# The first head's scores and exponentials are emitted beside the last projection, and the ring of exponentials moves into a pool that stays open

## The chip, the cores and the metric

The kernel runs on one core of one Trainium2 chip. The metric is device time in microseconds (us) of one launch. Instructions run on TensorE (PE, and PEld for its weight loads), VectorE (DVE), ScalarE (ACT) and GpSimd (POOL); SyncE (SP) issues nearly all transfers. Each engine runs its own instructions in order, and waits where an operand, a buffer or a transfer isn't ready.

## The reference, cut to what matters

```python
xn = rmsnorm(x, mix_norm);  proj = xn @ w_in          # 2 sequences x 512 tokens, 1024 -> 3072 columns
q, k, v, u = ...                                      # attention: 8 heads x 64; Hyena: 3 x 512 channels
q, k = rope(rmsnorm_f32(q, q_norm)), rope(rmsnorm_f32(k, k_norm))
attn = dilated_attention(q, k, v)                     # three (window, dilation) branches, merged by softmax
hy = hyena_mixer(u, ...)                              # short conv, then two gated long convolutions by FFT
mixed = concat(rmsnorm(attn), rmsnorm(hy));  h = x + mixed @ w_out
y = h + square(relu(rmsnorm(h, ffn_norm) @ w_up)) @ w_down
```

## The kernel before

All is float32 in value. A product is made of three matmuls of rounded halves (`hi`, `lo`), which `mm3` on line 91 emits; `act` on line 67 and `tt` on line 70 are the helpers under which most ACT and DVE work is recorded.

The first part of the program is written as Python generators which `interleave` merges by rough costs that each of them yields. One stream makes the filters of the Hyena group; two streams (`HA`, `HB`) run the Hyena convolutions, each as forward transforms (`psf`), a product on DVE (`t`, `yh`, `yl`), inverse transforms (`psi`) and a combination on DVE and POOL (`sm`, `wsb`, `u`, `z`); one stream runs the projections `proj_u` and `proj_qkv` (`psq`) and after them the attention; the last one turns the result of Hyena into `h` (`w_out_hyena`, `psm` and `psw`). A scheduler that knows the program's dependencies then fixes each engine's order.

The last projection is that of v for the second half of the heads (stream key `Q21`, `which` = 2, `half` = 1). Its q, k and v go to memory in DRAM (`q_d`, `k_d`, `v_d`). Only when it has ended are the pools `lw` and `la` (its weights and the normed input) closed, and `rm` and `lb` (attention) opened over their place: `start_attention` then loads the bias table, and `attn_load` loads q, k and v of a pair of heads (`qin`, `vin`).

For a head n = 2j + h, `stage_t` transposes its q and k (`psk`, 4 transposes each) and splits them (`qk`); `stage_a` makes the 128 x 512 scores of one tile of queries (`pss`, 2 matmuls), adds the bias and takes the maximum on DVE (`pe`, `mx`), and ACT makes exponentials in place; `stage_b` turns one block of keys (`psp`, 4 transposes, and `ph`, `pl`); `stage_v` multiplies by v (`pv`); `stage_c` turns the result back (`po`). `attention` runs five tiles of scores ahead of the rest:

```python
        for n in range(2):
            for k in range(2):
                stage_t(n, k)
        ...
        for t in range(5):
            scores()
```

Scores wait in a ring of eight buffers of 128 x 512 in `lb` (tag `pe`). When the second Hyena stream has stored its last result (`hy_d`), `w_out_hyena` loads it back in pieces (`hyr`), turns them (`psm`), and loads the weights of the output projection (`wur`).

Of the kernel before, what the change touches and what calls it, by code (L numbers as in the profile page):

```python
# [8 lines left out]
F32 = mybir.dt.float32  # L9
F32R = mybir.dt.float32r  # L10
# [45 lines left out]
def hybrid_encoder_kernel(ctx: ExitStack, tc: tile.TileContext, i: dict, outs, dbg=None):  # L56
# [74 lines left out]


    la, la_close = open_pool("la")
    lw, lw_close = open_pool("lw")
# [35 lines left out]
    def norm_x(s):  # L170
        for t in range(4):
            x = xs[s, t]
            c = slice(4 * s + t, 4 * s + t + 1)
            junk = [lw.tile([128, 512], F32, name="junk", tag=("y", "ut")[k], bufs=2) for k in range(2)]
            lo, hi = x[:, :512], x[:, 512:]
            nc.vector.tensor_tensor_reduce(out=junk[0], in0=lo, in1=lo, scale=1.0, scalar=0.0,
                                           op0=ALU.mult, op1=ALU.add, accum_out=rsc[:, 0, c])
            act(junk[1], hi, AF.Square, accum_out=rsc[:, 1, c])
            tt(nc.vector, ssx[:, c], rsc[:, 0, c], rsc[:, 1, c], ALU.add)
            rstd(ssx[:, c], ssx[:, c], D)  # L180
            act(hi, hi, AF.Copy, scale=ssx[:, c])
            nc.vector.tensor_scalar(lo, lo, ssx[:, c], None, op0=ALU.mult)
            yield 0, 1.2, 0
        for d in range(8):
            ps = bank("pst", "hx")
            for t in range(4):
                nc.tensor.transpose(ps[:, t * 128:(t + 1) * 128], xs[s, t][:, d * 128:(d + 1) * 128], ident)
            act(xh[s][:, d], ps, AF.Copy, scale=col(R_MIX + d))
            stt(xl[s][:, d], ps, col(R_MIX + d), f32(xh[s][:, d]), ALU.mult, ALU.subtract)
            if s == 0 and d == 3:  # L190
                load_x(1, nc.scalar, tc.keep_in_program_order)
            yield 0.43, 0.66, 0


    def load_w(src, first=False):

        out = []
        for k in range(src.shape[1]):
# [174 lines left out]
    def proj_u(q, w=None):  # L373
# [4 lines left out]
        def turn(s, a, y):  # L378
            pt = bank("pst", "tr", [128, 4, 128])
            for t in range(4):  # L380
                nc.tensor.transpose(pt[:, t], y[:, t * 128:(t + 1) * 128], ident)  # L381
            ut = lw.tile([128, 4, 128], F32, name="ut", tag="ut", bufs=2)
            act(ut, pt)
# [136 lines left out]
    def rope_tables():  # L520
        cs = lw.tile([128, 4, 2, 32], F32, name="cs", tag="y", bufs=2)
        nc.sync.dma_start(cs, i["c_rope"])
        g = lw.tile([128, 2, 64], F32, name="g", tag="ut", bufs=2)
# [4 lines left out]
        ng = lw.tile([128, 2, 64], F32, name="ng", tag="ut", bufs=2)  # L528
        nc.gpsimd.tensor_scalar(ng, g, -1.0, None, op0=ALU.mult)
# [8 lines left out]
    def proj_qkv(which, half):  # L538

        w = [(hi[:, c:c + 256], lo[:, c:c + 256]) for hi, lo in load_w(w_qkv[which, half]) for c in (0, 256)]  # L540
        for mp in range(4):
            s, t0 = divmod(2 * mp, 4)
# [8 lines left out]
            if which == 2:  # L551
# [3 lines left out]
                continue  # L555
            sq = lw.tile([128, 2, 256], F32, name="sq", tag="ut", bufs=2)
            rr = lw.tile([128, 8], F32, name="rr", tag="rr", bufs=3)
# [21 lines left out]

    ab = lw.tile([128, 4, 4, 64], F32, name="ab")  # L580
    w0 = load_w(w_u[0], first=True)
# [206 lines left out]
    PAIRS = [(s, 2 * g + p) for g in range(2) for s in range(NSEQ) for p in range(2)]  # L788
    split, po_of, den_of, sta, exps = {}, {}, {}, {}, {}

    def stage_t(n, k):


        j, h = divmod(n, 2)
        ps = bank("psk", "tr")
        for t in range(4):
            lined(nc.tensor.transpose(ps[:, t * 128:(t + 1) * 128], split[j][k][:, t, h], ident))  # L797
        hi = lb.tile([128, 512], F32R, name="qk", tag="qk", bufs=QKB)
        act(hi, ps)
# [3 lines left out]
        else:  # L803
            lo = lb.tile([128, 512], F32R, name="qk", tag="qk", bufs=QKB)
            tt(nc.vector, lo, ps, f32(hi), ALU.subtract)
            sta[n, k] = hi, lo

    def stage_a(n, t):

        j, h = divmod(n, 2)  # L810
        if t == 0:
            if h == 0:
                den_of[j] = lb.tile([128, 4, 2], F32, name="den", tag="den", bufs=2)
            exps[n] = [lb.tile([128, 4], F32, name="mx", tag="mx", bufs=3)]
# [5 lines left out]
        nc.vector.tensor_tensor_reduce(out=e, in0=ps, in1=bias[:, 384 - 128 * t:896 - 128 * t], scale=1.0, scalar=3e38,  # L820
                                       op0=ALU.add, op1=ALU.min, accum_out=mx[:, t:t + 1])
# [62 lines left out]
    def attention():  # L884
        load_pair(0)
        load_pair(1)
        for n in range(2):
            for k in range(2):
                stage_t(n, k)
                yield 0.4, 0.6, 0  # L890
        ahead = [(n, t) for n in range(NI) for t in range(4)]

# [4 lines left out]

        for t in range(5):
            scores()
            yield 0.47, 1.0, 0  # L900

# [29 lines left out]
    def w_out_hyena():  # L931
# [4 lines left out]
        for s in range(NSEQ):  # L936
# [6 lines left out]
            for t in range(4):  # L943
# [132 lines left out]
    w_out_part(1, between)  # L1076
    rm_close.close()
    hnB, hnB_close = open_pool("hnB")
    hn_pool(hnB, 1)
# [383 lines left out]
```

## Time and profile before

| | us |
|---|---|
| median of three runs (lowest, highest) | 1302.66 (1301.4, 1307.25) |
| the profiled execution, device time | 1303.84 |
| its span, first to last instruction | 1302.1 |
| PE busy in the span | 1263.6 (97%) |
| DVE, ACT, POOL busy | 1008.8, 658.5, 151.4 |

A busy PE is one with a matmul in flight; matmuls overlap, so the time between starts is the cost of one. Idle time of PE is mostly in three places: the first 60 us, the passage from the projections to the attention (432 to 480 us), and short gaps later. A row of the timeline merges equal instructions (x4) and ends, in brackets, with the idle time before them and what ended it.

### The profile page before, as it was taken

Reading aid. Unit: us, or ns where it says so; the run is one execution under the profiler, and the core shown is the slowest. Engines: PE = TensorE matmul, PEld = TensorE weight load, DVE = VectorE, ACT = ScalarE, POOL = GpSimd, SP = SyncE. Lnnn points to the kernel's source line nnn. Section 1 sums busy time; section 2 is a strip of 40 time slices with the busy share of each in tenths; the row PEclk is TensorE's granted clock in tenths of the full one; section 3 lists DMA queues with packets and bytes.
Section 4 is the critical chain, followed back from the end, with each engine's and each line's share of the span. In section 5 each row is a group of like instructions: output and inputs, shape, how many; then the busy total and the mean of one; then the engine's idle time right before and its main releaser. Section 6 shows DMA issues by size and latency. Waiting matters only on the chain.

```text
span 1302.1 us, 19021 instructions
## 1 busy us (share of the span) xinstructions
PE 1263.6 (97%) x6837; PEld 1079.8 (83%) x6837; DVE 1008.8 (77%) x1601; ACT 658.5 (51%) x1501; POOL 151.4 (12%) x131
## 2 busy tenths in 40 slices
PE   6999999999999889999999999999999999999998
PEld 5688889999999768788777888888887888887887
DVE  6787668898887777877569887887857688578885
ACT  6445434564564586768657444333335654334350
POOL 2110001443342130003031000000000000001000
PEclk9999999999999899999999999999999999999999
DMA  6545433444453494334232555444447853473323
GB/s 239 191 136 171 145 110 104 116 103 141 121 121 81 143 290 148 105 121 163 82 129 83 173 172 162 146 155 145 137 165 265 291 160 114 162 259 92 87 70 124
DMA packets 166275, 192.83 MB, mean 148 GB/s; under 512 B 42715, under 2 KB 106115, under 8 KB 166180
## 3 DMA queue, kind: packets, MB, share of 16 engines
q1 hardware_dynamic: 164740, 185.05, 45.0%
q0 software_dynamic: 864, 4.46, 0.9%
q10 hardware_dynamic: 576, 2.10, 0.4%
q8 instruction: 54, 0.88, 0.3%
q14 instruction: 41, 0.34, 0.1%
HBM read 126.82 MB, written 64.75 MB: 147 GB/s over the span
## 4 chain that ended last, share of the span: by engine, by line
PE 81%; DVE 9%; ACT 4%; DMA 3%; issue 2%; POOL 1%; SPq 0%; DVEq 0%; ACTq 0%; POOLq 0%
PE pu L91 24%; PE pn L91 19%; PE psu L91 10%; PE psq L91 6%; PE psw L91 5%; PE psf L91 4%; PE psi L91 3%; PE pv L845 2%; PE pss L818 2%; PE psp L831 2%; DVE clo L70 1%; DMA hyr<-hy_d 1%; PE pst L381 1%; DVE t L70 1%; PE psk L797 1%
## 5 line engine op out<-in xcount | busy, mean ns | idle before, releaser
L91 PE MATMUL pu<-hn,chl 128*128 128x512 f32 x768 | 184.6, 390 | 2.0 <-POOL hn L70 2.0
L91 PEld LDWEIGHTS pu<-hn,chl 128*128 128x128 f32 x768 | 144.2, 188 | 32.3 <-POOL hn L70 2.4
L91 PE MATMUL pn<-hn,chl 128*128 128x512 f32 x576 | 141.4, 392 | 1.0 <-ACT chl L67 1.0
L91 PEld LDWEIGHTS pn<-hn,chl 128*128 128x128 f32 x576 | 108.7, 189 | 24.8 <-ACT chl L67 1.9
L67 ACT ACTIVATE chi<-fa 128x1024 fp32r<-128x1024 f32 x49 | 51.9, 1060 | 124.4 <-PE pu L91 63.0
L91 PE MATMUL psq<-wlo,xh 128*128 128x256 f32 x384 | 108.8, 283 | 0.4 <-DVE wlo L70 0.4
L91 PE MATMUL psq<-whi,xl 128*128 128x256 f32 x384 | 108.7, 283 | 0.0
L91 PE MATMUL psq<-whi,xh 128*128 128x256 f32 x384 | 108.6, 283 | 0.0
L70 DVE TENSOR_TENSOR clo<-fa,chi 128x1024 fp32r<-128x1024 f32 x49 | 61.2, 1248 | 39.4 <-ACT chi L67 39.4
L91 PE MATMUL pu<-chi 128*128 128x512 f32 x248 | 86.6, 398 | 2.0 <-DVE chi L70 1.1
L91 PE MATMUL pu<-clo,chi 128*128 128x512 f32 x200 | 78.2, 391 | 1.6 <-DVE clo L70 1.6
L91 PE MATMUL pn<-chi 128*128 128x512 f32 x228 | 79.1, 389 | 0.0
L67 ACT ACTIVATE chl<-tmp 128x512 fp32r<-128x512 f32 x64 | 40.2, 630 | 76.0 <-PE pu L91 46.1
L91 PE MATMUL psu<-xh,whi 128*128 128x512 f32 x192 | 77.6, 407 | 0.5 <-ACT xh L67 0.5
L91 PE MATMUL pu<-chi,clo 128*128 128x512 f32 x200 | 77.8, 389 | 0.0
L91 PE MATMUL psf<-ih,dft 128*128 128x256 f32 x384 | 77.0, 283 | 0.2 <-ACT ih L67 0.2
L91 PE MATMUL psu<-xl,whi 128*128 128x512 f32 x192 | 76.7, 400 | 0.0
L91 PE MATMUL psu<-xh,wlo 128*128 128x512 f32 x192 | 76.1, 396 | 0.0
L91 PE MATMUL pn<-clo,chi 128*128 128x512 f32 x192 | 74.9, 390 | 0.1
L91 PE MATMUL pn<-chi,clo 128*128 128x512 f32 x192 | 74.7, 389 | 0.0
L91 PEld LDWEIGHTS psq<-wlo,xh 128*128 128x128 f32 x384 | 73.7, 192 | 0.6 <-DVE wlo L70 0.6
L91 PEld LDWEIGHTS psq<-whi,xh 128*128 128x128 f32 x384 | 73.7, 192 | 0.0
(243 smaller groups left out, 3201.5 us busy)
## 6 DMA issues: line engine op xcount, KB each, us to landing
fa<-f_d SPq DMA_DIRECT2D x49, 512.0 KB
wur<-in_w_up_t_dram SPq DMA_DIRECT2D x32, 512.0 KB
f_d<-x SPq DMA_DIRECT2D x60, 256.0 KB
wd<-in_w_down_dram SPq DMA_DIRECT2D x14, 1024.0 KB
f_d<-s SPq DMA_DIRECT2D x45, 256.0 KB
wraw<-in_w_u_dram SPq DMA_DIRECT2D x24, 256.0 KB
u_d<-ut SPq DMA_DIRECT2D x24, 256.0 KB
z<-u_d SPq DMA_DIRECT2D x24, 256.0 KB
```

The source lines that it names most:

```text
L67: nc.scalar.activation(out, in_, func, **kw)
L70: eng.tensor_tensor(out, a, b, op=op)
L91: pin(nc.tensor.matmul(ps, lhsT=w, rhs=x, start=start and k == 0, stop=stop and k == n - 1))
L381: nc.tensor.transpose(pt[:, t], y[:, t * 128:(t + 1) * 128], ident)
L797: lined(nc.tensor.transpose(ps[:, t * 128:(t + 1) * 128], split[j][k][:, t, h], ident))
L818: lined(nc.tensor.matmul(ps, lhsT=sta[n, 0][:, t * 128:(t + 1) * 128], rhs=kk, start=e == 0, stop=e == 1))
L831: lined(nc.tensor.transpose(ps[:, t * 128:(t + 1) * 128], exps[n][1 + t][:, kt * 128:(kt + 1) * 128], ident))
L845: lined(nc.tensor.matmul(pvs[n], lhsT=w, rhs=x, start=kt == 0 and e == 0, stop=kt == 3 and e == 1))
```

## The change

Head 0 is taken out of `attention` and given a stream of its own, `X`, with the generator `early`. It may start as soon as the last projection's weights are loaded (key `W21`). It loads q and k of heads 0 and 1 head by head (128 x 2 x 128 elements a transfer, where a pair's were 128 x 2 x 256), transposes head 0 and makes its four tiles of scores and exponentials. The bias is loaded twice: `bias0` for head 0 early, and `bias` as before. The attention's streams then begin with the transposes of head 1 and one tile of its scores. For pair 0, `attn_load` loads only v.

The buffers for this come from a new pool `le`, opened ahead of `la` and `lw`. It takes over the tags `wraw` (4 buffers), `ut` (2) and the table `ab` (the place of 2), and is closed only after the output projection. The ring of eight exponentials lies in these places (`exp_tile`), and the ring in `lb` is gone.

```diff
@@ pools
+    le, le_close = open_pool("le")
     la, la_close = open_pool("la")
@@ load_w
-                   lw.tile([128, 512], F32, name="wraw", tag="wraw", bufs=4))
+                   le.tile([128, 512], F32, name="wraw", tag="wraw", bufs=4))
...
@@ proj_qkv
+        done.add(f"W{which}{half}")
@@ attn_load
-        ins = []
-        for name, src in (("qin", q_d), ("qin", k_d)):
+        ins = [None, None] if (s, p) == PAIRS[0] else []
+        for name, src in (("qin", q_d), ("qin", k_d))[len(ins):]:
@@
+    def early():
+        bias0.append(le.tile([128, 896], F32, name="bias0", tag="ab", bufs=1))
+        den_of[0] = den0
+        for h in range(2):
+            for k, src in enumerate((q_d, k_d)):
+                t = le.tile([128, 4, 2, 64], F32, name="qin", tag="wraw", bufs=4)
+                for m in range(2):
+                    nc.sync.dma_start(t[:, 2 * m:2 * m + 2].rearrange("p t d e -> p t (d e)"),
+                                      src[m, :, 0, :, h].rearrange("p a d e -> p a (d e)"))
+                raws[h, k] = t.rearrange("p t d e -> p t (d e)")
+            if h == 0:
+                nc.sync.dma_start(bias0[0], i["c_bias"])
+        for k in range(2):
+            stage_t(0, k)
+            yield 0.4, 0.6, 0.6
+        for t in range(4):
+            stage_a(0, t)
+            yield 0.47, 1.0, 0.5
+
+    def exp_tile(i):
+        i %= 8
+        if i < 6:
+            tag, bufs = (("ut", 2), ("wraw", 4))[i > 1]
+            return le.tile([128, 512], F32, name="pe", tag=tag, bufs=bufs)
+        if i == 6:
+            two[:] = [le.tile([128, 2, 512], F32, name="pe", tag="ab", bufs=1)]
+        return two[0][:, i - 6]
@@ stage_a
-        ps = bank("pss", "ss")
+        ps = bank("pss", "ss" if n else "tr")
...
-        e = lb.tile([128, 512], F32, name="pe", tag="pe", bufs=8)
+        e = exp_tile(4 * n + t)
@@ attention
-        for n in range(2):
-            for k in range(2):
-                stage_t(n, k)
-                yield 0.4, 0.6, 0
-        ahead = [(n, t) for n in range(NI) for t in range(4)]
+        for k in range(2):
+            stage_t(1, k)
+            yield 0.4, 0.6, 0
+        ahead = [(n, t) for n in range(1, NI) for t in range(4)]
...
-        for t in range(5):
-            scores()
-            yield 0.47, 1.0, 0
+        scores()
+        yield 0.47, 1.0, 0
@@ streams
+        stream(("X", ("W21",), early())),
...
-               ("B", (), start_attention()), ("A", (), attention())),
+               ("B", ("X",), start_attention()), ("A", (), attention())),
@@ after the output projection
     rm_close.close()
+    le_close.close()
```

Outside the stretch that lies at about 360 to 500 us of the program before, every engine's order is the same as it was. Inside, it is another in three places of weight.

PE, from the end of the second Hyena stream's transforms; before, the transposes of heads 0 and 1 (16) and two tiles of scores stood ahead of the last inverse transform, and three tiles behind it:

```order
L91 MATMUL psi<-yh,dft 128x256
L797 MATMUL psk<-ident,qin 128x128 x16
L818 MATMUL pss<-qk 128x512 x4
L91 MATMUL psi<-yh,dft 128x256
L91 MATMUL psi<-yl,dft 128x256
L91 MATMUL psi<-yh,dft 128x256 x2
...
L818 MATMUL pss<-qk 128x512 x6
L831 MATMUL psp<-ident,pe 128x128 x4
L797 MATMUL psk<-ident,qin 128x128 x4
```

Of the change, the same place:

```order
L91 MATMUL psi<-yh,dft 128x256
L859 MATMUL pss<-qk 128x512 x2
L91 MATMUL psi<-yh,dft 128x256
L91 MATMUL psi<-yl,dft 128x256
L91 MATMUL psi<-yh,dft 128x256 x2
...
L872 MATMUL psp<-ident,pe 128x128 x4
L838 MATMUL psk<-ident,qin 128x128 x4
L859 MATMUL pss<-qk 128x512 x2
```

Only one tile of scores (head 1's first) is left there. Head 0's 8 transposes and 8 score matmuls now stand among the 192 `psq` matmuls of the last projection, and head 1's 8 transposes right behind its last one.

DVE, the end of the second Hyena stream (`z_3629` before, `z_3634` in the change); before:

```order
L70 TENSOR_TENSOR sm<-wsb,psi 128x512
L820 ISA pe,mx<-pss,bias 128x512
L820 ISA mx 128x1
L70 TENSOR_TENSOR wsb<-wsb,psi 128x512
L820 ISA pe,mx<-pss,bias 128x512
L820 ISA mx 128x1
L70 TENSOR_TENSOR u<-wsb,sm 128x256 x2
...
L73 SCALAR_TENSOR_TENSOR z_3629<-u,z_3629 128x256
L860 RECIPROCAL den<-den 128x4
L70 TENSOR_TENSOR pl<-psp,ph 128x512
L70 TENSOR_TENSOR z_3629<-z_3629,z_4466 128x1024
```

and of the change, from the copies of v (`v`, from `vin`) on:

```order
L70 TENSOR_TENSOR t_4884<-t_4884,t_4885 128x256 x2
L70 TENSOR_TENSOR v_5511<-vin,v_5511 128x8x64
L70 TENSOR_TENSOR yl<-t_4884,yh 128x512
L70 TENSOR_TENSOR sm<-wsb,psi 128x512
L70 TENSOR_TENSOR wsb<-wsb,psi 128x512
L70 TENSOR_TENSOR u<-wsb,sm 128x256 x2
L73 SCALAR_TENSOR_TENSOR z_3634<-u,wsb 128x256
L73 SCALAR_TENSOR_TENSOR z_3634<-u,z_3634 128x256
L70 TENSOR_TENSOR z_3634<-z_3634,z_4471 128x1024
L70 TENSOR_TENSOR pl<-psp,ph 128x512
```

The scores that stood between the steps of the combination are gone from there, and the second pair's copy of v stands ahead of `yl`, which the last inverse transform needs. ACT's order has the same: the second copy of v (`v_5511`), then `yh`.

SP, behind the last store of v; before:

```order
L554 DMA v_d<-qo 128x2x256 x4
L708 DMA bias<-in_c_bias_dram 128x896
L775 DMA qin<-q_d 128x2x256 x2
L775 DMA qin<-k_d 128x2x256 x2
L779 DMA vin<-v_d 128x4x128
L775 DMA qin<-q_d 128x2x256 x2
L779 DMA vin<-v_d 128x4x128
```

and of the change:

```order
L559 DMA v_d<-qo 128x2x256 x4
L713 DMA bias<-in_c_bias_dram 128x896
L784 DMA vin<-v_d 128x4x128
L780 DMA qin<-q_d 128x2x256 x2
L780 DMA qin<-k_d 128x2x256 x2
L784 DMA vin<-v_d 128x4x128
```

The first pair's four transfers of q and k are gone from here. Pair 0's v stands right behind the bias, pair 1's q and k behind it, and pair 1's v is the sixth transfer after the bias, where it was the eighth. Further up in SP's queue (not shown), the eight transfers of q and k for heads 0 and 1 stand among the last stores of q and k, and the first load of the bias behind them.

## Rows read from the trace of the kernel before

**Rows 1.** The page's first line.

```profile
span 1302.1 us, 19021 instructions
```

**Rows 2.** Busy time of each engine (us, instructions) in four stretches, then the granted clock of TensorE as a share of 2.4 GHz, the share of the DMA engines, and GB/s.

```profile
400.00:430.00 30.00, 30.00 (x252) 30.00 (x251) 21.57 (x33) 13.00 (x57) 9.26 (x9) 1.00 0.32 80
442.00:444.00 2.00, 1.44 (x8) 1.04 (x7) 1.08 (x2) 1.71 (x4) 0.00 (x0) 0.50 0.60 174
432.00:480.00 48.00, 36.91 (x206) 29.14 (x207) 36.98 (x83) 36.54 (x89) 13.08 (x11) 0.89 0.83 261
480.00:520.00 40.00, 40.00 (x225) 33.81 (x224) 31.32 (x68) 27.27 (x74) 0.00 (x0) 1.00 0.48 152
```

**Rows 3.** The timeline of PE in which one transpose group, one tile of scores and the next group follow each other: start, duration, engine, line, operation.

```profile
452.14 0.60 PE L797 MATMUL psk<-ident,qin 128*128 128x128 f32 x4
452.50 0.71 PE L818 MATMUL pss<-qk 128*128 128x512 f32 x2
453.04 0.60 PE L831 MATMUL psp<-ident,pe 128*128 128x128 f32 x4
```

**Rows 4.** The last projection: ACT's timeline where the Hyena stream's first input is split, and PE's where it is used.

```profile
415.01 1.23 ACT L67 ACTIVATE ih<-sd 128x512 fp32r<-128x512 f32 x2 [1.62 <-DVE sd L70]
...
418.39 0.28 PE L91 MATMUL psf<-ih,dft 128*128 128x256 f32 x1
```

**Rows 5.** PE's timeline from the end of the projection to the last inverse transform.

```profile
433.25 0.39 PE L91 MATMUL psi<-yh,dft 128*128 128x256 f32 x1 [1.25 <-ACT yh L67]
...
437.55 0.28 PE L91 MATMUL psi<-yh,dft 128*128 128x256 f32 x1
438.47 0.44 PE L797 MATMUL psk<-ident,qin 128*128 128x128 f32 x2 [0.65 <-DMA qin<-q_d]
439.19 0.44 PE L797 MATMUL psk<-ident,qin 128*128 128x128 f32 x2 [0.28 <-DMA qin<-q_d]
439.93 0.44 PE L797 MATMUL psk<-ident,qin 128*128 128x128 f32 x2 [0.30 <-DMA qin<-k_d]
441.57 1.54 PE L797 MATMUL psk<-ident,qin 128*128 128x128 f32 x6 [1.20 <-DMA qin<-k_d]
443.67 1.11 PE L797 MATMUL psk<-ident,qin 128*128 128x128 f32 x4 [0.56 <-DVE qk L70]
...
446.29 0.41 PE L91 MATMUL psi<-yh,dft 128*128 128x256 f32 x1
```

**Rows 6.** SP's timeline: when transfers are issued (the duration is that of the issue).

```profile
433.15 0.42 SPq L708 DMA_DIRECT2D bias<-in_c_bias_dram  x1
433.63 0.95 SPq L775 DMA_DIRECT2D qin<-q_d  x2
...
454.99 0.91 SPq L492 DMA_DIRECT2D hy_d<-z  x2
...
460.16 1.61 SPq L940 DMA_DIRECT2D hyr<-hy_d  x2
```

**Rows 7.** DVE's timeline around the last step of the second Hyena stream.

```profile
436.55 0.69 DVE L70 TENSOR_TENSOR z<-wsb,psi 128x512 f32<-128x512 f32 x1 [2.03 <-PE psi L91]
...
437.87 1.28 DVE L70 TENSOR_TENSOR t<-psf,hs 128x512 f32<-128x512 f32 x2
...
441.02 0.76 DVE L70 TENSOR_TENSOR t<-t,t 128x256 f32<-128x256 f32 x2
...
448.57 0.69 DVE L70 TENSOR_TENSOR sm<-wsb,psi 128x512 f32<-128x512 f32 x1 [0.49 <-PE psi L91]
449.17 0.68 DVE L820 CUSTOM_DVE_ANT_0 pe<-pss,bias 128x512 f32<-128x512 f32 x1
...
450.38 0.68 DVE L820 CUSTOM_DVE_ANT_0 pe<-pss,bias 128x512 f32<-128x512 f32 x1
...
451.81 0.68 DVE L820 CUSTOM_DVE_ANT_0 pe<-pss,bias 128x512 f32<-128x512 f32 x1
...
453.18 0.65 DVE L70 TENSOR_TENSOR pl<-psp,ph 128x512 fp32r<-128x512 f32 x1
453.76 1.21 DVE L70 TENSOR_TENSOR z<-z,z 128x1024 f32<-128x1024 f32 x1
```

**Rows 8.** ACT's timeline: the first copy of v, the table of the exponentials, one exponential and its sum.

```profile
442.79 0.62 ACT L67 ACTIVATE v<-vin 128x512 fp32r<-128x512 f32 x1
...
445.95 1.28 ACT L67 ACT_TABLE_LOAD   x1
447.25 0.72 ACT L67 ACTIVATE pe<-pe,mx 128x512 f32<-128x512 f32 x1
447.88 0.19 ACT L67 ACTIVATION_READ_ACCUMULATOR pe<-pe,mx 128x1 f32 x1
```

**Rows 9.** PE's timeline around the second piece of Hyena's result (`psm`).

```profile
465.53 0.63 PE L859 MATMUL po<-ident,ot 128*128 128x128 f32 x4 [0.25 <-DVE qk L70]
465.92 0.71 PE L818 MATMUL pss<-qk 128*128 128x512 f32 x2
468.58 1.12 PE L760 MATMUL psm<-ident,hyr 128*128 128x128 f32 x4 [1.95 <-DMA hyr<-hy_d]
...
470.35 1.05 PE L831 MATMUL psp<-ident,pe 128*128 128x128 f32 x4
471.06 0.97 PE L818 MATMUL pss<-qk 128*128 128x512 f32 x2
...
473.43 0.50 PE L845 MATMUL pv<-pl,v 128*128 128x512 f32 x1 [1.16 <-DVE pl L70]
```

More of the change, by code (lines that the diff above doesn't have):

```diff
@@ L122, in hybrid_encoder_kernel @@
     ssd = cp.tile([128, 2, 8], F32, name="ssd")
+    den0 = cp.tile([128, 4, 2], F32, name="den0")
+    mx0 = cp.tile([128, 4], F32, name="mx0")
     TAGS = {"ss": "mm", "pp": "hx"}
@@ L173, in norm_x @@
             c = slice(4 * s + t, 4 * s + t + 1)
-            junk = [lw.tile([128, 512], F32, name="junk", tag=("y", "ut")[k], bufs=2) for k in range(2)]
+            junk = [(lw, le)[k].tile([128, 512], F32, name="junk", tag=("y", "ut")[k], bufs=2) for k in range(2)]
             lo, hi = x[:, :512], x[:, 512:]
@@ L381, in turn @@
                 nc.tensor.transpose(pt[:, t], y[:, t * 128:(t + 1) * 128], ident)
-            ut = lw.tile([128, 4, 128], F32, name="ut", tag="ut", bufs=2)
+            ut = le.tile([128, 4, 128], F32, name="ut", tag="ut", bufs=2)
             act(ut, pt)
@@ L522, in rope_tables @@
         nc.sync.dma_start(cs, i["c_rope"])
-        g = lw.tile([128, 2, 64], F32, name="g", tag="ut", bufs=2)
+        g = le.tile([128, 2, 64], F32, name="g", tag="ut", bufs=2)
         for k, n in enumerate(("q_norm", "k_norm")):
@@ L527, in rope_tables @@
         nc.gpsimd.tensor_scalar(g[:, 0], g[:, 0], -0.125, None, op0=ALU.mult)
-        ng = lw.tile([128, 2, 64], F32, name="ng", tag="ut", bufs=2)
+        ng = le.tile([128, 2, 64], F32, name="ng", tag="ut", bufs=2)
         nc.gpsimd.tensor_scalar(ng, g, -1.0, None, op0=ALU.mult)
@@ L555, in proj_qkv @@
                 continue
-            sq = lw.tile([128, 2, 256], F32, name="sq", tag="ut", bufs=2)
+            sq = le.tile([128, 2, 256], F32, name="sq", tag="ut", bufs=2)
             rr = lw.tile([128, 8], F32, name="rr", tag="rr", bufs=3)
@@ L578, in proj_qkv @@
                 nc.sync.dma_start(dst[:, :, d], o3)
-    ab = lw.tile([128, 4, 4, 64], F32, name="ab")
+    ab = le.tile([128, 4, 4, 64], F32, name="ab", tag="ab", bufs=1)
     w0 = load_w(w_u[0], first=True)
@@ L789, in hybrid_encoder_kernel @@
     split, po_of, den_of, sta, exps = {}, {}, {}, {}, {}
+    raws, bias0, two = {}, [], []
+    def early():
[24 more added lines that the diff above has]
+        return two[0][:, i - 6]
     def stage_t(n, k):
@@ L795, in stage_t, with room @@
         ps = bank("psk", "tr")
+        def room(tag):
+            return (lw.tile([128, 512], F32R, name="qk", tag=tag, bufs=WB) if n == 0 else
+                    lb.tile([128, 512], F32R, name="qk", tag="qk", bufs=QKB))
         for t in range(4):
-            lined(nc.tensor.transpose(ps[:, t * 128:(t + 1) * 128], split[j][k][:, t, h], ident))
-        hi = lb.tile([128, 512], F32R, name="qk", tag="qk", bufs=QKB)
+            src = raws[n, k][:, t] if n < 2 else split[j][k][:, t, h]
+            lined(nc.tensor.transpose(ps[:, t * 128:(t + 1) * 128], src, ident))
+        hi = room("whi")
         act(hi, ps)
@@ L803, in stage_t @@
         else:
-            lo = lb.tile([128, 512], F32R, name="qk", tag="qk", bufs=QKB)
+            lo = room("wlo")
             tt(nc.vector, lo, ps, f32(hi), ALU.subtract)
@@ L811, in stage_a @@
         if t == 0:
-            if h == 0:
+            if h == 0 and j:
                 den_of[j] = lb.tile([128, 4, 2], F32, name="den", tag="den", bufs=2)
-            exps[n] = [lb.tile([128, 4], F32, name="mx", tag="mx", bufs=3)]
+            exps[n] = [lb.tile([128, 4], F32, name="mx", tag="mx", bufs=3) if n else mx0]
         den, mx = den_of[j], exps[n][0]
-        ps = bank("pss", "ss")
+        ps = bank("pss", "ss" if n else "tr")
         for e, kk in enumerate(sta[n, 1]):
             lined(nc.tensor.matmul(ps, lhsT=sta[n, 0][:, t * 128:(t + 1) * 128], rhs=kk, start=e == 0, stop=e == 1))
-        e = lb.tile([128, 512], F32, name="pe", tag="pe", bufs=8)
-        nc.vector.tensor_tensor_reduce(out=e, in0=ps, in1=bias[:, 384 - 128 * t:896 - 128 * t], scale=1.0, scalar=3e38,
+        e = exp_tile(4 * n + t)
+        nc.vector.tensor_tensor_reduce(out=e, in0=ps, in1=(bias if n else bias0[0])[:, 384 - 128 * t:896 - 128 * t], scale=1.0, scalar=3e38,
                                        op0=ALU.add, op1=ALU.min, accum_out=mx[:, t:t + 1])
```

## The prediction

> **What bounds the kernel now.** I first set PE's busy time beside the span: PE has a matmul in flight for 97% of 1302.1 us [rows 1], so only a stretch in which it waits, or runs at the lower clock, can give much back. The table by stretches shows where such a stretch lies: PE never rests from 400 to 430 us, rests 48.0 - 36.91 = 11.1 us from 432 to 480, and never rests from 480 to 520 [rows 2]. In the middle stretch the granted clock is 0.89 on average, and 0.50, which is 1.2 of 2.4 GHz, at 442 to 444 us. Eleven per cent of 36.9 us is some 4 us more, so the change can win 15 us at the very most, and it can move work only inside this stretch and the full one ahead of it.
>
> PE's timeline then tells what the 11 us are. The projection's last matmuls end at 432.0 (433.25 less the wait of 1.25); the inverse transforms go on to 437.8; then the 16 transposes of heads 0 and 1 wait in turn for q and k, 0.65 + 0.28 + 0.30 + 1.20 + 0.56 = 3.0 us, and the last inverse transform of Hyena starts only at 446.29, behind them [rows 5]. This transform matters for what comes after: DVE combines its result from 448.57 to about 455.0 [rows 7], SP stores it at 454.99, and the second piece that is read back (issued at 460.16) ends a wait of PE at 468.58 [rows 6, 9]. So the passage holds two chains: the attention's start, and Hyena's end with its way through DRAM. The second is still waited for at 468.
>
> **The change, step by step.** *Moved into the projection.* Four transposes take 452.50 - 452.14 = 0.36 us from start to start, one tile of scores 0.54 [rows 3]; head 0 is 8 transposes and 4 tiles, 0.7 + 2.2 = 2.9 us. As PE doesn't rest there, the end of the projection, and all that follows it, moves from its old time by +2.9. DVE gets two splits and three tiles of scores ahead of the next Hyena input, at 0.61 each [rows 7] some 3.0 us, so ACT's `ih` comes 3.0 later; it was ready at 416.2 and used at 418.39 [rows 4], 2.2 us of cover, and its user moves by 2.9 as well. That leaves 2.1 us and no stall. Without the cover each us more would be a us. ACT's table load (1.28) and four exponentials at 0.82 [rows 8] go into a stretch in which ACT is busy 13.00 of 30 us [rows 2]: nothing. The eight transfers of q and k stand on SP between stores and loads that wait for ACT or DVE themselves, with the DMA engines at 0.32 [rows 2]; the second copy of the bias (448 KB) lies there too: nothing.
>
> *Behind the projection.* Head 1's 8 transposes go into the wait of 1.25 us at 433.25 [rows 5]: 0.7 us, hidden. The inverse transforms that ended at 437.8 end at 440.7, and one tile of scores follows to 441.3. The waits for q and k, 3.0 us, are gone. What is late next? The last inverse transform stands next on PE, and nothing may overtake it. It needs `yh` and `yl`, and in the change both stand behind the copies of v. I follow DVE [rows 7]: `z` and `wsb` at 436.55 + 2.9 = 439.45, done at 440.8. The copy of pair 0's v is next. Its transfer now has the place behind the bias where the first q landed at 438.47 [rows 5], so 441.4; ACT's copy takes 0.62 [rows 8], DVE's part 0.6: 442.6. `t` 1.28, one tile of scores 0.6, `t` 0.76: 445.3. Then pair 1's v must have landed. No row shows this landing. It is the sixth transfer behind the bias; the fourth landed at 441.57 [rows 5], so 444.5 is the lower end; three transfers between 438.47 and 441.57 came 1.03 us apart, so two more make 446.5 the upper end. I take the middle, 445.5. ACT then copies v (0.62) and makes `yh` (0.6, as the copy): the transform starts at 446.7, which is 0.4 later than before, and between 445.9 and 447.7 over the bounds. PE has nothing from 441.3 until then.
>
> Here I weighed a rule. The rows give 1.03 us for 256 KB, when several transfers share the engines. The Trainium skill (DMA: Bandwidth & Descriptors, section Bandwidth) gives 6.15 us for 1 MB, 341 GB/s. By it the 2.2 MB from the last store of v to pair 1's v would have landed near 442.5 (an estimate from that page), `yh` would wait for DVE alone, and the sum below would be 0.8 us lower. I stay with the rows.
>
> *Hyena's end.* Between 448.57 and 455.0 DVE had three tiles of scores (0.61 each), a reciprocal and one `pl` (0.58) among the steps [rows 7]; they are gone from there, 2.5 us. So the combination takes 3.9 instead of 6.4 us: from 449.0 to 452.9. The store goes 2.1 us earlier. From the store to the landing of the second piece it was 468.58 - 454.99 = 13.6 us with the same transfers between them, so this lands at 466.5 instead of 468.6.
>
> *What follows it.* This is where the 2.1 us go. Before, `po` and a tile of scores were done ahead of the wait [rows 9]; in the change `psm` stands ahead of the last `psp` group, `po` and that tile, so PE does these after the landing: 0.44 + 0.39 + 0.54 = 1.4 us at full clock, 2.0 at half, as `psp` took 0.71 at 470.35 [rows 9]. DVE in its turn makes that tile's maximum and only then the `pl` for which the next `pv` waits, 1.2 us more, and has a `yl` (0.66) ahead of the following `pl`. Before, from `psm` at 468.58 to the late `pv` at 473.43 it was 4.85 us. In the change it is 4.85 + 1.4 + 1.2 + 0.7 = 8.1, less some 0.4 since the clock is back earlier: `pv` at 474.2. That is 0.8 late, but one further `psm` (0.36) is then done: +0.4. ACT's relief changes nothing here: of what it does after the transform, nothing could start sooner, since PE's transposes of the exponentials stand behind the transform.
>
> *Later.* PE doesn't rest from 480 on [rows 2], and the order is the old one: nothing. `le` is closed where `rm` is, and the last readers of its ring are long done: nothing.
>
> *The sum.* +2.9 of work ahead, -3.0 of waits for q and k, and the old waits that come back in other places make +0.4 us at the point where PE is full again; over the bounds of the landing -0.6 to +1.4, and half a us to either side for the clock. The profiled execution took 1303.84 (span 1302.1 and 1.7 around it), 1.2 over the median of the three runs. 1303.84 + 0.4 - 1.2 = 1303.0.
>
> **Rivals.** *The moved work comes straight off.* ACT and DVE are busy 36.5 and 37.0 of 48 us [rows 2], and 5.7 us of ACT's (four exponentials, table, two splits) and 3.7 of DVE's leave the stretch. If the attention's start is the longer chain, and the v transfers land early, PE is full again up to 5.7 us sooner: 1297. For it: the waits at 441.57 and 473.43 are of this chain. Against it: the last transform stands ahead of everything on PE. To win over 6.5 us (0.5% of 1302.66, about what a measurement of this kernel can tell from no change) the waits of both chains would have to go; filled wholly, it would be 1288.
>
> *Pair 1's v lands late, and the kernel gets slower.* PE waits for it at the last transform, and behind that wait are the exponentials' transposes, Hyena's store and all of `w_out_hyena`. Past 445.5 each us is a us. The loss passes 0.5% where the landing passes 451.6. For it: before, the second piece of Hyena's result took 8.4 us from 460.16 to its landing [rows 6, 9]; issued near 439, v would then land at 447.5 and the kernel take 1305. PE rests from 441.3 on, longer than at any wait in rows 5 and 9, and after the waits at 438 to 442 the clock was 0.50; at half rate until 452 it would lose 3 us more: 1308. The Trainium skill (TensorE: Matmul & The Clock Gate, What's actually happening) says that an idle engine falls back to 1.2 GHz; the trace agrees, with 0.50 at 442 to 444 behind those waits.
>
> *It doesn't do what it says*: head 0 stalls PE inside the projection, since DVE reaches its scores too late. The cover was 2.1 us; a loss of 1 to 3 us, 1304 to 1306.
>
> **Numbers.** The forecast has 0.58 (1301 to 1305 by itself); the moved work off, 2 to 6.5 us, 0.17, and more than that 0.09; v late or a stall in the projection, up to 6.5 us, 0.09, and more 0.07. Faster by over 0.5% 0.09, within it 0.84, slower 0.07. The range runs from 1297, where the gain of ACT's 5.7 us lies, to 1307.5: some 0.1 are left out on either side.
>
> **What would show it.** Right: `psk` for head 0 among `psq` with no wait; the last `psq` near 435; no `psk` that waits for `qin` behind it; one long rest of PE ahead of the last `psi`, ended by `yh`, itself behind a copy of v; the combination on DVE in about 4 us; `psm` again ended by `hyr`, near 466.5; PE full from about 480. Wrong: a `psi` that starts before 444.5, a wait for `hyr` that is gone, or new rests of PE before 432.

## The result, and the profile after the change

The change makes the kernel slower by 0.62%: 1311.69 us, median of 16 runs (1308.01 to 1314.2), against 1303.26 (1301.11 to 1307.25, 16 runs); ratio 1.0062, 95% interval 1.0054 to 1.0071. The forecast was 1303.0, with a range up to 1307.5. The execution that was profiled took 1314.2, the most of all 16, so its trace shows 2.5 us more than the median. The page's first line, which answers to [rows 1]:

```profile
span 1312.4 us, 19037 instructions
```

Starts of the same instructions in both traces say where the 10.3 us between the spans lie:

| start, us | before | after | difference |
|---|---|---|---|
| first `psq` | 210.1 | 209.2 | -0.9 |
| last `psq` | 431.7 | 432.5 | +0.8 |
| first `psw` on `yh` | 481.6 | 486.2 | +4.6 |
| first `pu` on `hn` | 671.2 | 676.3 | +5.1 |
| last `pu` on `hn` | 983.1 | 993.7 | +10.6 |
| end of the span | 1302.1 | 1312.4 | +10.3 |

So there are two losses. One lies where the change edits, 5.5 us in this execution: 1.7 in the projection (from -0.9 to +0.8) and 3.8 in the passage behind it, from the last `psq` to the first `psw` on `yh` (to +4.6). The other, 5.5 us too, lies in the up projection, 190 us behind it, where the prediction's term was "nothing".

**The passage.** The table by stretches for the change, columns as in [rows 2]:

```profile
400.00:430.00 30.00, 30.00 (x246) 29.63 (x245) 23.18 (x42) 16.79 (x57) 8.49 (x8) 1.00 0.39 113
432.00:480.00 48.00, 34.51 (x170) 28.51 (x170) 31.64 (x65) 28.19 (x70) 13.27 (x11) 0.72 0.77 245
442.00:455.00 13.00, 8.37 (x32) 7.40 (x33) 9.14 (x17) 4.86 (x19) 1.69 (x2) 0.51 0.37 106
466.00:480.00 14.00, 10.97 (x39) 8.87 (x40) 5.96 (x13) 8.38 (x19) 4.84 (x4) 0.51 1.00 341
480.00:520.00 40.00, 39.68 (x228) 33.20 (x226) 31.69 (x67) 27.51 (x73) 0.00 (x0) 1.00 0.39 126
```

PE still never rests from 400 to 430. From 432 to 480 it is busy 2.4 us less than before, at a clock of 0.72 instead of 0.89: two long pieces run at half clock, 442 to 455 and 466 to 480. Each stands behind a rest. These are PE's rows from the last `psq` on, and those around the second `psm`, which answer to [rows 5, 9]:

```profile
432.52 0.28 PE L91 MATMUL psq<-whi,xl 128*128 128x256 f32 x1
432.64 1.03 PE L838 MATMUL psk<-ident,qin 128*128 128x128 f32 x8
434.50 0.39 PE L91 MATMUL psi<-yh,dft 128*128 128x256 f32 x1 [0.82 <-ACT yh L67]
...
438.92 0.63 PE L859 MATMUL pss<-qk 128*128 128x512 f32 x2
444.74 0.58 PE L91 MATMUL psi<-yh,dft 128*128 128x256 f32 x1 [5.19 <-ACT yh L67]
...
463.60 0.40 PE L886 MATMUL pv<-pl,v 128*128 128x512 f32 x1
466.98 1.12 PE L765 MATMUL psm<-ident,hyr 128*128 128x128 f32 x4 [2.99 <-DMA hyr<-hy_d]
467.89 1.06 PE L872 MATMUL psp<-ident,pe 128*128 128x128 f32 x4
468.75 1.06 PE L900 MATMUL po<-ident,ot 128*128 128x128 f32 x4
469.46 1.20 PE L859 MATMUL pss<-qk 128*128 128x512 f32 x2
...
476.06 1.08 PE L765 MATMUL psm<-ident,hyr 128*128 128x128 f32 x4 [1.08 <-issue]
476.80 0.78 PE L886 MATMUL pv<-pl,v 128*128 128x512 f32 x1
```

The rest of 5.19 us is the one that was forecast. What stands ahead of its `yh` is seen on ACT and then on DVE, the rows that answer to [rows 7, 8]:

```profile
439.63 0.63 ACT L67 ACTIVATE v<-vin 128x512 fp32r<-128x512 f32 x1 [3.53 <-DMA vin<-v_d]
...
442.82 0.72 ACT L67 ACTIVATE pe<-pe,mx 128x512 f32<-128x512 f32 x1 [2.08 <-DVE mx L861]
443.45 0.19 ACT L67 ACTIVATION_READ_ACCUMULATOR pe<-pe,mx 128x1 f32 x1
443.54 0.63 ACT L67 ACTIVATE v<-vin 128x512 fp32r<-128x512 f32 x1
444.07 0.61 ACT L67 ACTIVATE yh<-t 128x512 fp32r<-128x512 f32 x1
```

```profile
438.53 0.69 DVE L70 TENSOR_TENSOR wsb<-wsb,psi 128x512 f32<-128x512 f32 x1
440.29 0.69 DVE L70 TENSOR_TENSOR v<-vin,v 128x512 fp32r<-128x512 f32 x1 [1.07 <-ACT v L67]
440.90 1.28 DVE L70 TENSOR_TENSOR t<-psf,hs 128x512 f32<-128x512 f32 x2
...
448.30 0.69 DVE L70 TENSOR_TENSOR sm<-wsb,psi 128x512 f32<-128x512 f32 x1 [2.81 <-PE psi L91]
```

Pair 0's v is what ACT waits for, 3.53 us, and DVE behind it; in front of the copy of pair 1's v, on whose landing the prediction had a bound, ACT doesn't rest.

**The up projection.** All matmuls on `hn` in the view by tile (count, shortest/median/longest ns, first and last start); of the kernel before, then of the change:

```profile
L91 PE MATMUL pu<-hn,chl x768: 388/389/618, 671.2 to 983.1; 128*128 128x512 f32 x192
```

```profile
L91 PE MATMUL pu<-hn,chl x768: 387/394/511, 676.3 to 993.7; 128*128 128x512 f32 x192
L91 PE MATMUL psw<-chl,mh x88: 392/394/502, 603.8 to 660.1; 128*128 128x512 f32 x88
```

The clock is 1.00 there in both, the count is the same, no new wait stands there; each matmul just takes longer. Taken from the starts, 1344 matmuls on `hn` follow each other every 226.7 ns before and every 231.1 ns after: 5.9 us. Those on `mh` go from 229.1 to 233.3. In the diff one thing reaches so far: two small tiles in the pool `cp`, which lies below every other pool of the left side. The cut diff ahead of the prediction doesn't show these two lines:

```diff
+    den0 = cp.tile([128, 4, 2], F32, name="den0")
+    mx0 = cp.tile([128, 4], F32, name="mx0")
```

With their alignment they take 64 bytes a partition, and in the built program `hnB` (the second half of `hn`) starts at byte 17952 instead of 17888.

### The profile page after: what moved, and what is told of

Read it like the earlier page. It is cut to its first block, busy times and chain, and to the rows that moved or that the text cites. A ratio compares the mean times of both kernels' runs of the same rounds, so it can differ in the third digit from the quotient of the medians.

```text
span 1312.4 us, 19037 instructions
## 1 busy us (share of the span) xinstructions
PE 1270.6 (97%) x6837; PEld 1081.0 (82%) x6837; DVE 1010.2 (77%) x1601; ACT 659.8 (50%) x1501; POOL 151.7 (12%) x131
## 4 chain that ended last, share of the span: by engine, by line
PE 80%; DVE 9%; ACT 4%; DMA 3%; issue 2%; POOL 1%; SPq 0%; DVEq 0%; ACTq 0%; POOLq 0%
PE pu L91 24%; PE pn L91 19%; PE psu L91 10%; PE psq L91 6%; PE psw L91 5%; PE psf L91 4%; PE psi L91 3%; PE pv L886 2%; PE pss L859 2%; PE psp L872 2%; DVE clo L70 1%; DVE t L70 1%; PE pst L385 1%; DMA tmp<-f_d 1%; PE psk L838 1%
## 5 line engine op out<-in xcount | busy, mean ns | idle before, releaser
L91 PE MATMUL pu<-hn,chl 128*128 128x512 f32 x768 | 187.8, 394 | 1.9 <-POOL hn L70 1.9
L91 PE MATMUL pn<-hn,chl 128*128 128x512 f32 x576 | 144.1, 397 | 0.8 <-ACT chl L67 0.8
```

What stands on the lines that cost most here:

```text
L91: pin(nc.tensor.matmul(ps, lhsT=w, rhs=x, start=start and k == 0, stop=stop and k == n - 1))
```

## The experiments

Ratios are against runs of the kernel before on the same chip; 0.1% is 1.3 us.

| run | what it is | median, us | ratio, 95% interval |
|---|---|---|---|
| e1 | before, + 64 bytes | 1308.23 | 1.0040 (1.0028 to 1.0052) |
| e2 | change, 128 bytes in all | 1312.62 | 1.0074 (1.0061 to 1.0087) |
| e3 | change, `hnB` at its old place | 1307.49 | 1.0029 (1.0018 to 1.0041) |
| e4 | change, rest filled | 1309.17 | 1.0041 (1.0029 to 1.0053) |
| e5, e6 | before, `hnB` 256 and 512 higher | 1302.21, 1303.01 (one run each) | |
| e7 | all tiles placed, `psm` order | 1305.64 | 1.0015 (1.0004 to 1.0027) |
| e8 | the same, rest filled | 1303.35 | 0.9992 (0.9982 to 1.0003) |
| e9, e10 | v late, without and with fill | 1305.59, 1303.72 | 1.0018 (1.0005 to 1.0031), 1.0002 (0.9990 to 1.0015) |
| e11, e12 | the same, `psm` by hand | 1307.09, 1306.84 | 1.0030 (1.0021 to 1.0039), 1.0027 (1.0016 to 1.0038) |
| e13, e14 | v late, `hyr` first, without and with fill | 1304.28, 1302.73 | 1.0006 (0.9995 to 1.0017), 0.9997 (0.9987 to 1.0008) |

### Placement: e1, e2, e3, e5, e6

```diff
@@ e1, on the kernel before
-    ssd = cp.tile([128, 2, 8], F32, name="ssd")
+    ssd, _ = cp.tile([128, 2, 8], F32, name="ssd"), cp.tile([128, 16], F32, name="pad")
@@ e2, on the change
-    mx0 = cp.tile([128, 4], F32, name="mx0")
+    mx0, _ = cp.tile([128, 4], F32, name="mx0"), cp.tile([128, 16], F32, name="pad")
@@ e3, on the change; the two lines in cp are gone
     le, le_close = open_pool("le")
+    den0 = le.tile([128, 4, 2], F32, name="den0")
+    mx0 = le.tile([128, 4], F32, name="mx0")
@@ e5, and e6 with 128 for 64, on the kernel before
+    gap, gap_close = open_pool("gap"); gap.tile([128, 64], F32, name="pad")
     hnB, hnB_close = open_pool("hnB")
```

> The kernel before, with one unused tile of 64 bytes a partition beside `ssd`, so that every tile of the pools opened after `cp` on the left side lies 64 bytes higher, as `den0` and `mx0` do it in the change; nothing else differs. Theory A (placement): in the trace of the change the matmuls of pu and pn that read hn start 231 ns apart and before 226.7 ns apart, 1344 of them, some 5.9 us, and those of psw that read mh and ml 233 instead of 229, 0.7 us; the shift of hnB and mh is the cause. Then this kernel takes 1303.3 + 6.5 = 1309.8, with pu<-hn,chl at a mean of 394 ns and the way from the first pu<-hn to the last 5 us longer than before. Theory B (the transition at 430 to 480 us holds the whole loss, and the pace of the up projection is an accident of one execution): 1303.3, no difference, 390 ns.

> The change, with one more unused tile of 64 bytes a partition beside `mx0`, so that the tiles above `cp` on the left lie 128 bytes, not 64, higher than in the kernel before. Theory A with the place within 128 bytes as what counts: the matmuls on hn are back at 389 to 390 ns, and the kernel takes 1311.7 - 6.5 = 1305.2. Theory A with any other place than the old one as slow: 394 ns and 1311.7. Theory B: 1311.7, whatever the ns.

> The change, with `den0` and `mx0` in the pool `le` instead of `cp`. `hnB`, which is opened after `le` is closed, then lies where it lay before; `mh` and `ml`, above `le`, lie where they lie in the change. Every engine's order of instructions is that of the change. Theory A: pu and pn on hn back at 390 ns, psw on mh still at 394; 1311.7 - 5.9 = 1305.8, and what is left over 1303.3 is the transition's. Theory B: 1311.7.

Of e1 and then of e3, the view by tile:

```profile
L91 PE MATMUL pu<-hn,chl x768: 387/394/628, 670.9 to 988.2; 128*128 128x512 f32 x192
```

```profile
L91 PE MATMUL pu<-hn,chl x768: 387/389/632, 670.0 to 981.8; 128*128 128x512 f32 x192
L91 PE MATMUL psw<-chl,mh x88: 391/394/505, 597.4 to 653.8; 128*128 128x512 f32 x88
```

Theory A held in all three (in e2 its second reading, that any place but the old one is slow). An unused tile of 64 bytes costs the kernel before 0.40%, 5.2 us, and stretches the way from the first `pu` on `hn` to the last from 311.9 to 317.3 us. With `hnB` back at its place the change has 311.8 us and is 0.33% quicker, while `mh`, which stayed shifted, stays at 394 ns. The engines' orders are the same in e3 as in the change, so the order doesn't set this pace. 128 bytes (e2) are no better: 230.6 ns from start to start.

> The kernel before, with an unused tile of 256 bytes opened right ahead of `hnB`: only the seven pairs of tiles hn of the second half lie 256 bytes higher, nothing else moves. In the kernel before, hn of both halves and the weights' halves chl start at addresses that leave the same remainder by 512 (480); in the change, and in the two shifts by 64 and 128 tried so far, hn of the second half left another one. Theory A1 (what counts is that the operands leave the same remainder by 512): the matmuls on hn take 230 ns or more from start to start, and the time is some 5 us above before. Theory A2 (the same remainder by 256, or less, is enough): 226.7 ns, and no difference in time.

> The same with 512 bytes. A1 and A2: 226.7 ns and the time of before. Theory A3 (only the very old place is a good one, or more than 512 counts): 231 ns and 5 us more.

The matmuls on `hn` start 226.7 and 226.8 ns apart, so A2 holds as far as it was tried: at both places `hn` of the second half leaves the remainder by 256 which `hn` of the first half and the weights `chl` have (224 in the built program), and the pace is the old one; 64 and 128 bytes off it the starts lie 2% further apart. Which pair of the three has to agree was not taken apart, nor were distances other than these, and the two times are of one execution each.

### The passage: e4, e7, e8

e3 shows one thing more. Each engine's order is that of the change, but the execution that was profiled is the fastest of e3's six (1303.0 us), and the change's is the slowest of 16. In e3's trace, the second `psm` and the late `pv` which in the change start at 466.98 and 476.80, and the stretch from 466 to 480:

```profile
464.96 0.66 PE L765 MATMUL psm<-ident,hyr 128*128 128x128 f32 x4 [1.84 <-DMA hyr<-hy_d]
471.81 0.50 PE L886 MATMUL pv<-pl,v 128*128 128x512 f32 x1
```

```profile
466.00:480.00 14.00, 11.25 (x69) 8.61 (x68) 12.02 (x26) 12.97 (x30) 3.99 (x4) 1.00 1.06 347
```

The clock stays at 1.00 behind this shorter rest, and the same instructions take 6.9 us instead of 9.8. Their waits are no shorter (the two that are left over 0.3 us are 1.16 and 1.27, in the change 0.97 and 1.08), so 3.0 us is what the half clock costs there. The order of instructions doesn't fix whether the clock falls. The passage from the last `psq` to the first `psw` takes 47.6 us in e3's trace, 53.7 in the change's and 49.9 before: the 3.8 us that the first table has for it are those of one execution, the longest.

```diff
@@ e4 and e8, attention
         scores()
+        ps = bank("pfill", "tr")
+        for _ in range(16):
+            lined(nc.tensor.matmul(ps, lhsT=sta[1, 0][:, :128], rhs=sta[1, 1][0], start=True, stop=True))
         yield 0.47, 1.0, 0
@@ e7 to e14, instead of the two lines in cp
+    den0 = ssd[:, 0].rearrange("p (t h) -> p t h", h=2)
+    mx0 = ssd[:, 1, :4]
@@ e7, attention; held[0] is the first psm of Hyena's second piece
                 if scores():
+                    if (n, t) == (1, 2):
+                        tc.add_manual_dep(held[0].ins, chain[0], mybir.DependencyInfo(
+                            mybir.DependencyClass.NoSync, mybir.DependencyReason.DATA))
```

> The change, with 16 matmuls of 512 columns whose result nobody reads put on PE between head 1's first tile of scores and Hyena's last inverse transform, where PE rests 5.2 us in the change (439.6 to 444.7). They take 16 x 0.227 = 3.6 us of that rest. Theory C (the rest costs through the clock: 0.50 from 445 to 455): the granted clock stays at 1.00 past 445, psi takes some 2 us instead of 3.5, Hyena's store goes some 2 us earlier, and the kernel gains 2 us: 1309.7. Theory D (the half clock there is off the path that sets the end, which waits for DVE and for the store's way through DRAM): the clock stays up, and the time is 1311.7. The scheduler also moves the transposes of hyr behind some of the attention's work in this build, so the stretch after 460 is read from the trace by itself.

> The change with two edits: `den0` and `mx0` lie in `ssd`, which nobody uses by then, so that all tiles lie as before or a multiple of 512 bytes from there (theory A: pu and pn on hn at 226.7 ns, psw on mh at 229); and on PE the transposes psm of Hyena's second piece stand behind the last psp group, po and a tile of scores, as in the kernel before, instead of ahead of them. Against the run with den0 in le (1307.5): theory E (the order behind the landing of hyr costs what the prediction had for it, 1.4 on PE and 1.2 on DVE): 0.5 for mh and 2.6 for the order less, 1304.4. Theory C (the clock is what costs, the order nothing): 1307.0, with half clock in the passage as in the change.

> The same place for `den0` and `mx0`, and the 16 unread matmuls ahead of the last inverse transform; the scheduler then orders psm of the second piece as in the kernel before. Theory C: the filled rest is worth some 2 us more than the order alone, 1302.4 if both count, 1304.4 if the order counts nothing and the placement is 5.2 (1309.2 - 5.2 = 1304.0). Theory D (the half clock is off the path): the same as with the order alone.

e4 is 0.21% quicker than the change, as theory C had it, but its order of `psm` differs from the change's too; e7 and e8 were to part the two. They have the same placement and the same place of the second `psm`. Beside the 16 unread matmuls they differ in what the scheduler made of them: in e8 the first `psm` stands one score matmul and one `pv` later, and the load of the third piece ahead of one of `hq`. The stretches 442 to 455 and 466 to 480 of e7, of e8, then of e4:

```profile
442.00:455.00 13.00, 8.06 (x32) 7.14 (x33) 8.67 (x17) 4.65 (x17) 1.69 (x2) 0.61 0.34 100
466.00:480.00 14.00, 8.54 (x49) 6.42 (x48) 10.29 (x22) 11.41 (x27) 5.19 (x5) 0.96 1.01 339
```

```profile
442.00:455.00 13.00, 9.01 (x39) 7.62 (x37) 8.45 (x18) 3.75 (x7) 1.69 (x2) 0.66 0.31 93
466.00:480.00 14.00, 11.72 (x70) 8.74 (x70) 11.62 (x26) 14.00 (x33) 7.20 (x6) 1.00 1.08 363
```

```profile
442.00:455.00 13.00, 9.68 (x47) 7.99 (x47) 9.72 (x19) 4.19 (x8) 1.69 (x2) 0.87 0.42 126
466.00:480.00 14.00, 11.89 (x69) 8.47 (x67) 12.19 (x26) 13.98 (x33) 6.50 (x6) 1.00 1.08 363
```

e7's 1305.64 lies between theory E's 1304.4 and C's 1307.0. Work that nobody reads, put into PE's rest, makes the kernel faster: 1.0015 without, 0.9992 with it, 3.0 us (2.3 between the medians), and the intervals miss each other by 0.0001. So D, which had no difference, is unlikely. C is borne out by the whole span: the granted clock, as a mean of 12 executions, is 0.9927 in e7 and 0.9952 in e8 (0.9942 over the 23 of the kernel before), and 0.0025 of the span is 3.3 us. It is not borne out at the place that it names: behind the filled rest the clock is 0.66 in e8's trace and 0.61 in e7's, and only in e4's trace did it stay up (0.87). Where the two traces part is the fourth `psm`, of e7 and then of e8:

```profile
478.94 1.08 PE L765 MATMUL psm<-ident,hyr 128*128 128x128 f32 x4 [3.54 <-DMA hyr<-hy_d]
```

```profile
477.04 0.66 PE L765 MATMUL psm<-ident,hyr 128*128 128x128 f32 x4 [0.40 <-DVE yl L73]
```

That the fill is worth 2 to 3 us is measured; that it works through the clock is likely; in which stretch is open. What the order of `psm` is worth lies between e3 and e7, 1.8 us with 0.5 for `mh` in it; those intervals overlap, so that share is likely but not settled.

### Hyena's chain: e9 to e14

Here ACT's copies of v for pairs 0 and 1 are held back behind the first `ph`, so that they no longer stand ahead of the last `yh`. e10, e12 and e14 have 8 unread matmuls as well. In e11 to e13 the first two `psm` are put in their places by hand, as e7 does it. In e13 and e14 the loads of the output weights depend on the first `hyr` (`back`).

```diff
@@ e9 to e14, attn_load and stage_b
-        act(v2[:, :, :, 0], ins[2])
-        tt(nc.vector, v2[:, :, :, 1], ins[2], f32(v2[:, :, :, 0]), ALU.subtract)
+        def copy(after=None):
+            head = nc.scalar.activation(v2[:, :, :, 0], ins[2], AF.Copy)
...
+        late.append(copy) if (s, p) in PAIRS[:2] else copy()
...
+        head = nc.scalar.activation(ph, ps, AF.Copy)
+        while late:
+            late.pop(0)(head)
@@ e13 and e14, w_out_hyena
-        wo = w_out_weights(1)
...
+                wo = wo or w_out_weights(1, back)
```

> `den0` and `mx0` in `ssd`, no fill, and the copies of v of pairs 0 and 1 held back on ACT until the first `ph`, so that neither stands ahead of the last `yh`. In the change DVE has finished `wsb` at 439.22, then waits for ACT's copy of pair 0's v, and starts `t` at 440.90; pair 1's copy on ACT costs 0.53 more ahead of `yh` at 444.07. Theory F (v's copies set when the last inverse transform starts): `t` starts at 439.2, `yh` 2.2 us earlier, the transform at some 442.3 instead of 444.7, Hyena's store 2.4 earlier; as the rest is half as long, the half clock is shorter as well; against 1307.0 for the same placement without it (1307.5 with den0 in le, less 0.5 for mh) some 3 us less, 1304.0. Rival (the exponential and `mx` on ACT and DVE set it): the transform at 444, 1306.5. The scheduler puts psm of the second piece behind a tile of scores in this build.

> The same with 8 unread matmuls (8 x 0.227 = 1.8 us) ahead of the last inverse transform, which fill what the later copies of v leave of the rest (some 2.5 us). Theory C with F: no half clock, or 3.4 us of it, from 440 to 460, and 2 us less than without the fill: 1302.0, below the kernel before (1303.8). Rival (the passage is bound by Hyena's store and its way back through DRAM, so that neither counts): 1303.5 as with 16 unread matmuls and v's copies in front.

In e9 the transform starts at 443.19, 9.9 us behind the last `psq`, where it was 12.2 in the change: 2.3 us earlier, theory F's 2.4. The time is not 1304.0 but 1305.59, no better than e7, and e10 has 1303.72 where 1302.0 was expected, no better than e8. In e9 the scheduler moved the first `psm` to 466.26, from 457.96 in the change. So two runs put it back by hand.

> `den0` and `mx0` in `ssd`, v's copies held back, no fill, and the first two pieces of Hyena (psm) put by hand where the kernel before has them on PE: the second one behind po and a tile of scores. Against the same order with v's copies in front (1305.6): theory F: the last inverse transform starts 2.4 us earlier after the projection's last psq, and Hyena's store with it; 1303.2. Rival (the passage is not bound by this transform): 1305.6.

> The same with 8 unread matmuls ahead of the last inverse transform. Theory C with F: the half clock is gone or short in 440 to 460 us, and 2 us less than without the fill, 1301.2, below the kernel before (1303.4) and the fill with v's copies in front (1303.35). Rival: both make the same stretch shorter, and 1303.2 stays.

Both missed. e12 is slower than e10; e11 is slower than e9 by its median, but the intervals overlap. PE's timeline in e12, and SP's:

```profile
464.74 1.11 PE L764 MATMUL psm<-ident,hyr 128*128 128x128 f32 x4 [7.75 <-DMA hyr<-hy_d]
```

```profile
451.17 0.91 SPq L496 DMA_DIRECT2D hy_d<-z  x2
452.38 1.09 SPq L785 DMA_DIRECT2D vin<-v_d  x2
453.56 2.66 SPq L755 DMA_DIRECT2D wur<-in_w_out_dram  x4
456.26 1.22 SPq L993 DMA_DIRECT2D hyr<-hy_d  x2
```

The store left 2.0 us earlier than in the change (453.13), but four loads of output weights, 2 MB, had slipped between it and the first `hyr`. PE waited 7.75 us for that. In e13 and e14 the loads stand behind it again.

> As e11 (den0 and mx0 in `ssd`, v's copies held back, psm's places by hand, no fill), and on SP the loads of the output weights stand behind the first hyr, as in the kernel before. Theory F: Hyena's store 2.4 us earlier after the projection's end than in e7, the first psm without a long wait, and 1305.6 - 2.4 = 1303.2. Rival (the transform's start does not set the passage): 1305.6. If the loads on SP weren't what made e11 slow: 1307.1.

> The same with 8 unread matmuls ahead of the last inverse transform; the order of PE from there on is that of e8 and of the kernel before. Theory C with F: 1301.3, below the kernel before (1303.4). Rival: 1303.4, as e8.

By the ratios e13 gains 1.2 us on e7, where 2.4 were expected, and the intervals overlap; e14 gains nothing that can be told on e8. Why the earlier store is worth so little is seen in e14: SP's timeline, the row of 455 to 465 us from the table by stretches, and PE's timeline:

```profile
451.06 0.91 SPq L496 DMA_DIRECT2D hy_d<-z  x2
452.28 1.09 SPq L787 DMA_DIRECT2D vin<-v_d  x2
453.42 0.68 SPq L990 DMA_DIRECT2D hyr<-hy_d  x1
454.15 2.07 SPq L755 DMA_DIRECT2D wur<-in_w_out_dram  x4
456.27 1.14 SPq L990 DMA_DIRECT2D hyr<-hy_d  x1
```

```profile
455.00:465.00 10.00, 8.32 (x47) 6.44 (x47) 6.71 (x17) 8.03 (x19) 5.75 (x5) 0.92 1.03 333
```

```profile
466.81 0.66 PE L768 MATMUL psm<-ident,hyr 128*128 128x128 f32 x4 [1.42 <-DMA hyr<-hy_d]
```

The second piece ends its wait at 466.81, 15.75 us behind the store; in the change it was 466.98, 13.85 behind one that left 2.1 us later. From 455 to 465 the DMA engines are full, with 1.03 of their time at 333 GB/s, as they are from 466 to 480 in the rows above (1.00 to 1.08). And the queue in front of the second piece has grown: the two loads of v behind the store, 0.5 MB, left ahead of it in the change (441.01 and 444.92). They fill the two buffers that the first two pairs' v leave, and these come free only when the copies of v, now held back, have run. So the edit that sent the store earlier also put 0.5 MB between it and the landing, and e9 to e14 don't show what an earlier store alone is worth. e14 and e8, the best of all variants, are level with the kernel before; none beats it.

## Why the prediction was wrong, step by step

**"Later: PE doesn't rest from 480 on, and the order is the old one: nothing"** is the step that failed most. Order and rests were indeed the old ones, but a matmul's duration is not fixed by them. The diff's two lines in `cp` were never costed. By e1 they cost 5.2 us, by e3 4.3 are won back without them: more than half of the 8.1.

**"Less some 0.4 since the clock is back earlier"**, with half a us to either side for the clock, is the second. From the second `psm` to the late `pv` I had 466.5 to 474.2, 7.7 us; it was 466.98 to 476.80, 9.8 us, at 0.51 of the clock, and 6.9 us in e3's trace, at 1.00. So the work was sized about right, and the clock was not: it can fall behind each of the two rests that are left, and in the change's trace it did so twice. I priced the rest of 5.4 us, which I had worked out myself, as a wait only. Its cost in clock, 3 us, stood among the rivals, tied there to a late v that did not occur; 3.0 us is what the traces of e3 and of the change differ by in this one stretch. The Trainium skill (TensorE: Matmul & The Clock Gate, What's actually happening), cited there, has an idle engine fall to 1.2 GHz; the trace agrees, with 0.51 behind the rest of 5.19 us and again behind that of 2.99. Behind e3's rest of 1.84 us the clock stayed at 1.00.

**What held.** Head 0's matmuls stand among `psq` without a wait, and PE is busy 30.00 of 30 us. The projection is longer by 1.8 us in this execution (223.4 instead of 221.6 from the first `psq` to the last) and in e3's, and by 3.0 in e7's, 2.9 forecast. Head 1's `psk` went into the wait for `yh`, 0.82 of which is left; the waits for q and k are gone. The rest was forecast as 441.3 to 446.7 and is 439.6 to 444.7, ended by `yh` behind a copy of v. The copy that was late was pair 0's, 7.1 us behind the start of the last `psq` where I had 6.8 (441.4 less 431.7 and 2.9). Pair 1's v had landed at 443.51, by the last update of its semaphore in the trace: 9.59 us behind the issue of the bias (433.92), where the rows had given 9.45 (445.5 less 433.15 and 2.9). By the Trainium skill's 341 GB/s (DMA: Bandwidth & Descriptors, Bandwidth) I had estimated 442.5, which is 6.45. The trace agrees with the rate, since the six transfers behind the bias landed 0.80 us apart, 328 GB/s, and not with the estimate: the bias itself, 448 KB, landed 4.8 us behind its issue. The landing ended no wait all the same, as ACT was busy with an exponential until then. DVE's combination took 4.8 us (448.30 to 453.11) and not 3.9; the store went 1.9 us earlier and the second piece landed 1.6 earlier, where 2.1 and 2.1 were forecast.

**The sum** of the change's own steps was +0.4. With `hn` at its old place they come to +3.8 (e3, interval 2.3 to 5.3), 0.5 of it the pace on `mh`. What is left over the forecast, 2.9, is of the size of the clock's 3.0; that it is the same us is not shown, since e3's trace is of its fastest execution. e13 comes near the forecast (+0.8, interval -0.7 to +2.2), but with another order and with v's copies held back, so it doesn't bear the forecast out. Moving head 0 into the projection gives nothing in itself: PE has no rest there that it could fill, and behind it one long rest is left.

## What to carry to other kernels

When a diff adds even a small tile ahead of long-lived pools, compare the addresses of the matmul operands before and after, and add the pace of the matmuls far behind the edit to what is priced; a small tile belongs where nothing lies above it. When work is taken out of a stretch with waits, price the rest that it leaves twice, as a wait and as the clock behind it. And do not carry a delay from a store to a landing over as a constant: look at what the queue puts in between.

## What the runs showed of the hardware that was not expected

- Matmuls of 512 columns in float32r halves start 226.7 ns apart when both halves of `hn` and the weights leave the same remainder by 256 bytes, and 231.1 or 230.6 ns apart when one half of `hn` lies 64 or 128 bytes off (e1, e2); 256 and 512 bytes off they start 226.7 and 226.8 ns apart (e5, e6). The granted clock from 700 to 980 us is 1.00 in all of them.
- In the change the matmuls on both halves of `hn` are slower, though only one half moved: 231.5 ns from start to start on the half that stayed, 230.7 on the one that moved.
- In the change the clock was 0.51 from 442 to 455 us, though PE worked again from 444.74; with that rest filled it was 0.87 in e4's trace and 0.66 in e8's.
- With one and the same order of every engine's instructions the clock from 466 to 480 us was 0.51 in one execution (the change, 1314.2 us) and 1.00 in another (e3, 1303.0 us).
